# Padding the SBUF pools of a hybrid encoder block so that the tiles of its 128x512 matmuls start at multiples of 128 bytes

## The chip, the cores and the metric

The kernel runs on one core of one Trainium2 chip. The metric is the device time of that core in microseconds (us). The core's engines are TensorE (PE in the rows; its weight loads are listed as PEld), VectorE (DVE), ScalarE (ACT), GpSimd (POOL) and SyncE (SP, which here only issues transfers). Tiles live in SBUF, 128 partitions wide; a tile's address is the byte at which it starts in each partition, and that byte is what this change is about. Matmul results go to PSUM.

## What is computed

One layer of a streaming encoder over `x` of 2048 tokens and 1024 channels, all in float32 (cut):

```python
xn = rmsnorm(h, in_norm_g)
q, fz, v, gz, u = split(xn @ w_in)             # 2560 columns
o_hg = hgrn2_mix(q, fz, v, gz, lb, norm_g)     # gated linear recurrence, 4 heads, chunks of 64
o_s5 = s5_mix(u, ...)                          # 32 groups of a 64-state complex SSM, then a GLU of 512x512
h = h + concatenate([o_hg, o_s5]) @ w_out
hn = rmsnorm(h, ffn_norm_g)
hid = hn @ w_up                                # 1024 -> 2 * 2816
hid = conv_b + sum(shifted(hid, j) * conv_w[j] for j in range(3))
gate, val = split(hid)
h = h + (silu(gate) * val) @ w_down            # 2816 -> 1024
return rmsnorm(h, final_norm_g)
```

## The kernel before

**Matmuls.** Every large product is done in split precision: a float32 tile is written as a high part (`ACTIVATE`, line 121) and a low part (a subtraction, line 65), both of type `float32r`, and three matmuls replace one: high x high, high x low, low x high. Each of them is a 128x128 weight block against 512 moving columns. The program has 8,448 of these 128x512 matmuls. They are issued in one fixed order, and each loads its own weights:

```python
for kt in range(KT):                                         # project, lines 216 to 222
    a = wh[:, kt * P : (kt + 1) * P]                         # weights, high
    b = wl[:, kt * P : (kt + 1) * P]                         # weights, low
    xh, xl = xn[0][kt // 4][:, kt % 4], xn[1][kt // 4][:, kt % 4]
    PE.matmul(ps, a, xh, start=(kt == 0), stop=False)        # L220: weights, then moving tile
    PE.matmul(ps, a, xl, start=False, stop=False)            # L221
    PE.matmul(ps, b, xh, start=False, stop=(kt == KT - 1))   # L222
```

**Stages**, in order of time:

- *Projection and mixers* (0 to about 640 us). `project` (L220 to L222) makes 80 blocks of 24 matmuls: weights `wh`, `wl` of pool `wp`, moving tiles `xh`, `xl` of pool `xnp`. Between the blocks stand short float32 matmuls of the two mixers (L489, L574, L575, L637, L681, L700, L702 and others, up to 128 columns), with their DVE, ACT and POOL work and their transfers. The list `todo` ties each mixer step to a block ("slot").
- *GLU and output projection* (640 to 865 us). `glu_mm` (L886 to L888) has weights `wg` and moving tiles `g`, both in pool `wop`; `out_tile` (L963) has weights `ogp` and `zp` (pool `mx`) and moving tiles `wo` (pool `wop`), 16 tiles of 48 matmuls.
- *Up-projection with convolution* (about 870 to 1760 us). 44 units (2 token halves x 22 feature pairs) of seven Strassen-like products P1 to P7, 12 matmuls each, by `product` (L1162). The weights `uh`, `ul` (pool `fw`) are made while the unit before runs. The moving tiles are the token sums: P1 and P2 read `nh`, `nl` (pool `fa`), the other five read `tT1`, `tT2`, `tB22`, `tT3`, `tT4` (pool `fb`). In 40 units the order is P1, P5, P6, P2, P7, P3, P4, so that P5 (`tT1`) and P7 (`tT3`) stand right behind the two that read `nh`, `nl`.
- *Down-projection* (about 1770 to the end). 96 x 2 plain matmuls (`down`, L1466) and then 20 chunks of seven products of 24 matmuls (`one_product`, L1379): weights `gvh`, `gvl` (pool `fd`), moving tiles `dh`, `dl` (half of them in `fa`, half in `fd`). After each product DVE adds PSUM to the accumulator `accp` (line 62); behind that, in DVE's order, it makes the `gvl` and `dl` of the next chunk (line 65) from `graw`, which is loaded from `gv_d`.

**What sets addresses.** Tiles are taken from pools. A pool lies on the left (addresses rise) or, with `side="right"`, on the right, below the one opened before it. A tile takes its size, rounded up to 32 bytes, and there is no other rounding. So one odd-sized small tile shifts all that follows it in its pool, and the pools behind it. The right side starts at byte 229,344, which is 1,791 x 128 + 96: the four 4,096-byte buffers of `xp`, and what lies below them, start 96 bytes past a multiple of 128. The lines that matter:

```python
cp = ctx.enter_context(tc.tile_pool(name="cp", bufs=1))                       # 90
sm = ctx.enter_context(tc.tile_pool(name="sm", bufs=2))                       # 91
xp = ctx.enter_context(tc.tile_pool(name="xp", bufs=4, side="right"))         # 92
lbm = cs.tile([P, 4], F32, name="lbm")                                        # 303: 16 bytes, takes 32
sf = p3.enter_context(tc.tile_pool(name="sf", bufs=2))                        # 1272: small tiles, ahead of fd
```

## Time and profile before

| | us |
|---|---|
| three runs | 2249.85, 2245.22, 2246.74 (median 2246.74) |
| the profiled execution | 2248.36 |
| its span, first to last instruction | 2246.5 |
| PE busy in the span | 2163.2 (96%), 10,248 instructions |
| DVE busy | 1700.3 (76%) |
| ACT busy | 994.9 (44%) |
| POOL busy | 732.3 (33%) |
[...]

The span leaves 1.9 us of the profiled execution outside it. A PE that is busy 96% is not yet at its peak: the durations of matmuls overlap (a row gives about 0.39 us for a matmul whose successor starts after 0.23 us), so what a matmul costs is read from the distance between starts, or from a piece of the chain of waits, which counts no time twice.

### The profile page before, as it was taken

Reading aid. Unit: us, or ns where it says so; the run is one execution under the profiler, and the core shown is the slowest. Engines: PE = TensorE matmul, PEld = TensorE weight load, DVE = VectorE, ACT = ScalarE, POOL = GpSimd, SP = SyncE. Lnnn points to the kernel's source line nnn. Section 1 sums busy time; section 2 is a strip of 40 time slices with the busy share of each in tenths; the row PEclk is TensorE's granted clock in tenths of the full one; section 3 lists DMA queues with packets and bytes.
Section 4 is the critical chain, followed back from the end, with each engine's and each line's share of the span. In section 5 each row is a group of like instructions: output and inputs, shape, how many; then the busy total and the mean of one; then the engine's idle time right before and its main releaser. Section 6 shows DMA issues by size and latency. Waiting matters only on the chain.

```text
span 2246.5 us, 28693 instructions
## 1 busy us (share of the span) xinstructions
PE 2163.2 (96%) x10248; PEld 1745.3 (78%) x10248; DVE 1700.3 (76%) x2629; ACT 994.9 (44%) x1818; POOL 732.3 (33%) x666
## 2 busy tenths in 40 slices
PE   8999999999989998999999999999999889999996
PEld 6788887888878886888878877888888667777775
DVE  9998885666673336877778798777777788788888
ACT  5333462333363346655555564555555323232343
POOL 1111100000000001555455546565544245354433
PEclk9999999999999999999999999999999999999998
DMA  6566665354433357334324252222221622222223
GB/s 225 167 209 190 195 194 168 108 159 126 142 113 113 113 170 239 122 113 136 121 91 145 79 191 96 82 78 84 75 85 57 241 92 80 75 85 76 75 85 122
DMA packets 169519, 287.37 MB, mean 128 GB/s; under 512 B 46112, under 2 KB 85920, under 8 KB 169376
## 3 DMA queue, kind: packets, MB, share of 16 engines
q1 hardware_dynamic: 164624, 268.23, 37.0%
q0 software_dynamic: 4752, 17.30, 2.0%
q8 instruction: 81, 1.33, 0.2%
q14 instruction: 62, 0.51, 0.1%
HBM read 191.11 MB, written 94.37 MB: 127 GB/s over the span
## 4 chain that ended last, share of the span: by engine, by line
PE 70%; DVE 17%; DMA 5%; issue 4%; ACT 3%; SPq 1%; POOL 1%; DVEq 0%; POOLq 0%; ACTq 0%
PE ps_u L1162 18%; PE ps_v L1162 9%; PE ps_out L963 7%; PE ps_du L1379 5%; PE ps_w L1162 5%; PE ps_pj L220 5%; PE ps_pj L222 5%; PE ps_pj L221 5%; PE ps_dv L1379 3%; DVE accp L62 2%; DVE gvl L65 2%; DMA graw<-gv_d 2%; DVE dl L65 1%; PE ps_dn L1466 1%; DVE cv L74 1%
## 5 line engine op out<-in xcount | busy, mean ns | idle before, releaser
L220 PE MATMUL ps_pj<-xh,wh 128*128 128x512 f32 x640 | 261.9, 409 | 6.5 <-ACT xh L190 6.3
L222 PE MATMUL ps_pj<-xh,wl 128*128 128x512 f32 x640 | 255.1, 399 | 0.5 <-DMA wl<-ws_d 0.5
L221 PE MATMUL ps_pj<-xl,wh 128*128 128x512 f32 x640 | 255.5, 399 | 0.0
L74 DVE SCALAR_TENSOR_TENSOR cv<-cv,par 128x1024 f32<-128x1024 f32 x176 | 238.5, 1372 | 19.8 <-ACT cv L1174 17.8
L121 ACT ACTIVATE uh<-us 128x512 fp32r<-128x512 f32 x176 | 110.5, 629 | 183.2 <-PE ps_u L1162 87.8
L56 POOL TENSOR_TENSOR us<-uraw 128x512 f32<-128x512 f32 x86 | 122.1, 1420 | 186.7 <-DMA uraw<-in_wup_dram 170.0
L121 ACT ACTIVATE uh<-uraw 128x512 fp32r<-128x512 f32 x132 | 83.4, 632 | 159.7 <-PE ps_u L1162 84.4
L1379 PE MATMUL ps_du<-dh,gvh 128*128 128x512 f32 x320 | 131.6, 411 | 22.8 <-DVE accp L62 16.5
L65 DVE TENSOR_TENSOR ul<-us,uh 128x512 fp32r<-128x512 f32 x133 | 150.3, 1130 | 1.4 <-ACT uh L121 1.3
L220 PEld LDWEIGHTS ps_pj<-xh,wh 128*128 128x128 f32 x640 | 121.3, 189 | 37.2 <-ACT xh L190 6.3
L222 PEld LDWEIGHTS ps_pj<-xh,wl 128*128 128x128 f32 x640 | 121.1, 189 | 30.1 <-DMA wl<-ws_d 0.9
L221 PEld LDWEIGHTS ps_pj<-xl,wh 128*128 128x128 f32 x640 | 121.3, 190 | 26.9 <-DVE xl L74 0.9
L65 POOL TENSOR_TENSOR ul<-us,uh 128x512 fp32r<-128x512 f32 x43 | 72.8, 1692 | 174.4 <-ACT uh L121 174.4
L1379 PE MATMUL ps_du<-dl,gvh 128*128 128x512 f32 x320 | 127.9, 400 | 0.0
L1379 PE MATMUL ps_du<-dh,gvl 128*128 128x512 f32 x320 | 127.9, 400 | 0.0
L121 ACT ACTIVATE gvh<-gs 128x512 fp32r<-128x512 f32 x80 | 50.4, 630 | 161.6 <-POOL gs L56 77.0
L62 DVE TENSOR_TENSOR accp<-accp,ps_du 128x1024 f32<-128x1024 f32 (+1 forms) x84 | 97.7, 1163 | 28.0 <-PE ps_du L1379 27.7
L1174 ACT ACTIVATE cv<-cv,par 128x1024 f32<-128x1024 f32 x88 | 109.5, 1244 | 16.3 <-DVE cv L62 14.9
L56 POOL TENSOR_TENSOR gs<-graw 128x512 f32<-128x512 f32 x38 | 58.9, 1549 | 157.2 <-DMA graw<-gv_d 157.2
L963 PE MATMUL ps_out<-wo,ogp 128*128 128x512 f32 x384 | 100.2, 409 | 0.0
L1379 PEld LDWEIGHTS ps_du<-dh,gvh 128*128 128x128 f32 x320 | 61.5, 192 | 46.8 <-issue 23.1
L963 PE MATMUL ps_out<-wo,zp 128*128 128x512 f32 x384 | 92.7, 397 | 0.0
(431 smaller groups left out, 6024.8 us busy)
## 6 DMA issues: line engine op xcount, KB each, us to landing
uraw<-in_wup_dram SPq DMA_DIRECT2D x86, 512.0 KB
gv_d<-cv SPq DMA_DIRECT2D x43, 512.0 KB
graw<-gv_d SPq DMA_DIRECT2D x84, 256.0 KB
wraw<-in_win_dram SPq DMA_DIRECT2D x24, 512.0 KB
xt<-in_wdown_dram SPq DMA_DIRECT2D x44, 256.0 KB
ws_d<-wh POOLq DMA_DIRECT2D x16, 512.0 KB, 3.8
ws_d<-wl POOLq DMA_DIRECT2D x16, 512.0 KB, 5.7
wh<-ws_d SPq DMA_DIRECT2D x16, 512.0 KB
```

Source lines behind the costliest of these rows:

```text
L56: eng.tensor_tensor(o, a, b, op=op)
L62: eng.tensor_tensor(o, a, b, op=ALU.add)
L65: eng.tensor_tensor(o, a, b, op=ALU.subtract)
L74: eng.scalar_tensor_tensor(o, a, s, b, op0=op0, op1=op1)
L121: SC.activation(h, raw, AF.Copy)
L220: PE.matmul(ps, a, xh, start=(kt == 0), stop=False)
L221: PE.matmul(ps, a, xl, start=False, stop=False)
L222: PE.matmul(ps, b, xh, start=False, stop=(kt == KT - 1))
L963: PE.matmul(pss[nh], parts[lp][kt][:, tq], wo[rp][kt][:, nh * BLK : (nh + 1) * BLK], start=first, stop=last)
L1162: PE.matmul(ps, l, r[kt], start=(fresh and first), stop=end, skip_group_check=not fresh)
L1174: SC.activation(c, cin[:, 2 : HALF + 2], AF.Identity, scale=tap[2], bias=par[:, C_CB + cb : C_CB + cb + 1])
L1379: PE.matmul(ps[:, i], l[:, j, i * P : (i + 1) * P], r, start=(fresh and n == 0), stop=(n == 5), skip_group_check=not fresh)
```

## The change

Five small tiles that nobody reads or writes are allocated, one at each place where a pool would leave the multiples of 128. They are 96 bytes at the top of the right side, 64 in `sp`, 32 and 64 in `cs`, and 64 in `sf`. No other line changes.

```diff
+LINE, TOP = 128, 229344
+
+
 def _body(ctx, tc, A, out, dbg=None):
...
     sm = ctx.enter_context(tc.tile_pool(name="sm", bufs=2))
+    top = ctx.enter_context(tc.tile_pool(name="top", bufs=1, side="right"))
+    top.tile([P, (TOP - LINE * (TOP // LINE)) // 4], F32, name="pad")
     xp = ctx.enter_context(tc.tile_pool(name="xp", bufs=4, side="right"))
...
         sp = p1.enter_context(tc.tile_pool(name="sp", bufs=1, side="right"))
+        sp.tile([P, 16], F32, name="pad")
         hp = p1.enter_context(tc.tile_pool(name="hp", bufs=1, side="right"))
...
         lbn = cs.tile([P, 4], F32, name="lbn")
+        cs.tile([P, 8], F32, name="pad")
...
         r8 = cs.tile([P, PAIRS], F32, name="r8")
+        cs.tile([P, 16], F32, name="pad2")
         nci = cs.tile([P, PAIRS, 16], F32, name="nci")
...
         sf = p3.enter_context(tc.tile_pool(name="sf", bufs=2))
+        sf.tile([P, 16], F32, name="pad", bufs=1)
         fd = p3.enter_context(tc.tile_pool(name="fd", reuse_waits="tile", bufs=1))
```

No instruction moves: on each engine the built program has the same instructions in the same order with the same operands and shapes, and the same waits, but for one wait of POOL that is content with one ACT instruction fewer. Only addresses differ. The start of the 128x512 matmuls' operands, in bytes past a multiple of 128, as the two builds lay them out:

| line | matmuls | moving tile: before, after | weight block: before, after |
|---|---|---|---|
| L220, L221, L222 (projection) | 1,920 | 0, 0 | 32, 0 |
| L886 to L888 (GLU) | 192 | 0, 0 | 0, 0 |
| L963 (output projection) | 768 | 0, 0 | 96, 0 |
| L1162, P1 and P2 (`nh`, `nl`) | 1,056 | 96, 0 | 0, 0 |
| L1162, the other five products | 2,640 | 0, 0 | 0, 0 |
| L1379 (down-projection) | 1,680 | 64 or 96, 0 | 64, 0 |
| L1466 (plain down-projection) | 192 | 96, 0 | 64, 0 |

That L1162 has two rows is what makes it useful: 1,056 matmuls whose moving tile is off, and 2,640 with both operands on a multiple of 128, run in turn in the same stage. The short float32 matmuls of the mixers have operands at 32 or 96 before, and at 0 after in all but a few. The tiles of the convolution (`cv`, six buffers of 4,104 bytes) are not brought to multiples of 128, only shifted.

## Rows read from the trace of the kernel before

**Rows 1.** Windows, all engines: stretch, length, busy us (instructions) per engine, granted clock.

```profile
core 0: us, PE busy (x) PEld busy (x) DVE busy (x) ACT busy (x) POOL busy (x), PEclk, DMA share, GB/s
0.00:100.00 100.00, 86.28 (x396) 66.79 (x397) 90.41 (x332) 43.30 (x76) 13.77 (x49) 0.97 0.63 202
100.00:350.00 250.00, 248.27 (x1566) 204.15 (x1565) 221.98 (x565) 113.42 (x292) 26.64 (x71) 1.00 0.62 193
350.00:640.00 290.00, 286.46 (x1678) 236.04 (x1678) 185.09 (x430) 97.03 (x281) 3.65 (x17) 1.00 0.43 133
1360.00:1740.00 380.00, 379.15 (x1650) 309.54 (x1649) 284.32 (x257) 192.32 (x274) 206.48 (x156) 1.00 0.24 79
1820.00:2180.00 360.00, 345.97 (x1460) 275.07 (x1460) 300.09 (x321) 114.92 (x192) 157.16 (x102) 0.99 0.23 74
```

**Rows 2.** Waits of PE over the span: total us, times, longest.

```profile
PE ps_du L1379 <- DVE accp L62: 16.5, 18, 4.6
...
PE ps_u L1162 <- DVE cv L62: 5.4, 3, 3.7
...
PE ps_du L1379 <- DVE rs_t L59: 2.6, 1, 2.6
```

**Rows 3.** Chain of waits, 1400 to 1425 us: start, us, what.

```profile
1400.62 2.76 PE ps_u L1162 x12
1403.38 2.72 PE ps_v L1162 x12
1406.10 5.53 PE ps_u L1162 x24
...
1417.11 2.81 PE ps_w L1162 x12
```

**Rows 4.** Lines of PE, 700 to 760 us: xcount, busy us, mean ns.

```profile
L963 PE MATMUL ps_out<-wo,ogp 128*128 128x512 f32 x98 | 23.8, 396 | 0.0
...
L887 PE MATMUL ps_glu<-g,wg 128*128 128x512 f32 x22 | 8.6, 389 | 0.0
```

**Rows 5.** Chain of waits, 640 to 830 us.

```profile
703.96 22.49 PE ps_out L963 x96
```

**Rows 6.** Timeline of PE, 560 to 567 us: start, us, instruction.

```profile
563.52 0.39 PE L221 MATMUL ps_pj<-xl,wh 128*128 128x512 f32 x1
...
566.78 0.40 PE L220 MATMUL ps_pj<-xh,wh 128*128 128x512 f32 x1
```

**Rows 7.** Timeline of PE behind a short wait, 1341.9 to 1345.3 us.

```profile
1342.31 0.50 PE L1162 MATMUL ps_u<-tT3h,uh 128*128 128x512 f32 x1
1342.65 0.40 PE L1162 MATMUL ps_u<-tT3l,uh 128*128 128x512 f32 x1
...
1345.21 0.40 PE L1162 MATMUL ps_u<-nh,uh 128*128 128x512 f32 x1
```

**Rows 8.** Windows of L221 alone: stretch, length, busy us (instructions) of PE, PEld.

```profile
100.00:350.00 250.00, 95.58 (x241) 45.18 (x240) 1.00 0.62 193
350.00:640.00 290.00, 117.10 (x296) 55.71 (x296) 1.00 0.43 133
```

**Rows 9.** Chain of waits, 1896 to 1926 us.

```profile
1898.38 5.55 PE ps_du L1379 x24
```

**Rows 10.** Chain of waits, 2082 to 2104 us.

```profile
2082.22 3.34 DMA graw<-gv_d
...
2088.03 1.23 DVE gvl L65
...
2094.57 3.00 PE ps_du L1379 x12
```

**Rows 11.** Chain of waits, 2170 to 2181 us.

```profile
2176.22 4.56 PE ps_du L1379 x12
```

**Rows 12.** Lines of ACT, 900 to 2180 us: xcount, busy us, mean ns.

```profile
L121 ACT ACTIVATE uh<-us 128x512 fp32r<-128x512 f32 x169 | 106.1, 629 | 179.7 <-PE ps_u L1162 87.8 <-PE ps_w L1162 68.1 <-PE ps_v L1162 23.6
...
L121 ACT ACTIVATE gvh<-gs 128x512 fp32r<-128x512 f32 x75 | 47.3, 631 | 156.1 <-POOL gs L56 73.0 <-PE ps_du L1379 35.1 <-DVE gs L56 22.8
```

## The prediction

> **What bounds the kernel now.** I read the windows first. PE is busy 248.27 of 250 us in the second part of the projection stage, 286.46 of 290 in its third and 379.15 of 380 in the up-projection; DVE, the next engine, is busy 89%, 64% and 75% there [rows 1]. Then the list of PE's waits: in a span of 2246.5 us the longest entry is 16.5 us, for DVE's accumulation in the down-projection, and the up-projection's largest is 5.4 us [rows 2]. So over most of the time the end is set by how fast PE starts one matmul after the other. A change of addresses moves no instruction; what it can change is the distance between two starts.

> That distance is in the chain of waits, where a piece with a count holds so many matmuls back to back. In the up-projection the trace compares addresses by itself, since P1 and P2 read `nh`, `nl` (96 bytes past a multiple of 128) and the rest read tiles that lie on one. The 12 matmuls of P2 (`ps_w`) take 2.81 us, 234.2 ns each. The 12 of P3 (`tB22`, the `ps_v` piece) take 2.72 us, 226.7 ns each. P7, right behind P2, reads `tT3`, which lies on a multiple of 128, and takes 2.76 us, 230.0 ns each (the first `ps_u` piece) [rows 3]. I read the last as an after-effect: starts that fell out of step take most of a product to fall back in. Of 24 matmuls in one piece (P4, then P1 of the next unit) 5.53 us are 12 x 226.7 + 12 x 234.2 [rows 3], so the two prices add up.

> Weights count too. In the output projection and GLU all moving tiles are on multiples of 128, and weights are on one for L887 but 96 past one for L963: mean durations 389 and 396 ns [rows 4], and 96 matmuls of L963 take 22.49 us, 234.3 ns each [rows 5]. Projection, weights 32 past: 14 distances from 563.52 to 566.78 us, 232.9 ns each [rows 6]. Down-projection, both operands off: 24 in 5.55 us, 231.2 ns [rows 9]. Every group with an operand off costs 231 to 234 ns, the groups with none 226.7. I take 226.7 ns as the price after.

> **The change part by part.** It adds no work, so the sum is one of gains, matmuls x (price now - 226.7 ns), cut where PE does not set the pace.

> *Up-projection.* P1 and P2: 2 x 12 x 44 = 1,056 matmuls x 7.5 ns = 7.9 us. P5 and P7 lose their after-effect: 12 x (230.0 - 226.7) = 40 ns, in some 82 products, 3.3 us. PE sets the pace here (379.15 of 380 us, [rows 1]). A unit gets shorter by 2 x 90 + 2 x 40 = 0.26 us of 19.3, 1.3%, and DVE at 75% covers that. I take 11.0 of 11.2, for the few products at the start that wait.

> *Output projection.* 768 matmuls x (234.3 - 226.7) = 5.8 us. The last quarter is woven with transposes and waits for transfers; I count 592 matmuls in full (4.5 us) and 0.3 for the rest: 4.8.

> *Projection.* Each block of 24 follows short float32 matmuls. Behind a break the next starts are slow even with both operands on multiples of 128: the first distance is 0.34 us, and from 1342.65 to 1345.21 us follow 11 of 232.7 ns [rows 7]. So only the later 12 of 24 gain, 12 x 6.2 = 74 ns a block. From 350 us on, 296 / 8 = 37 blocks [rows 8]: 2.7 us, kept, with DVE at 64%. From 100 to 350 us, 241 / 8 = 30 blocks, 2.2 us; DVE is 89% busy, so I keep 1.4. Before 100 us PE is busy 86 and DVE 90 [rows 1], and PE follows loads and splits: 0. Together 4.1.

> *Down-projection.* Of a chunk's 84 matmuls some 22 stand behind one of two breaks; 62 x (231.2 - 226.7) = 0.28 us, times 20 = 5.5 us. Here another loop is close. `graw` is loaded (3.34 us) after DVE has released its buffer, then POOL, ACT and DVE work on it, and PE waits for the accumulation queued behind that in DVE's order [rows 10]. Where a chunk has this stall, a faster PE only waits longer, and there are 18 such waits over the 20 chunks [rows 2]. I keep a little under half, 0.45 x 5.5 = 2.4, for the chunks between two stalls in which DVE has caught up. The 192 plain matmuls: 192 x 4.5 = 0.9, kept.

> *Short float32 matmuls.* 632 starts of 128 columns with operands off. If the price goes with columns, 7.5 / 4 = 1.9 ns each, 1.2 us; if it is per start, 4.7; if nothing, 0. I take 0.8, near the first, since part lies under DVE.

> *Other engines.* ACT's split takes 629 ns for tiles on a multiple of 128 (`uh`) and 631 for tiles 64 past one (`gvh`) [rows 12]: no price there, so I cost ACT, DVE and POOL at 0. I have no row that sets a load's address against its duration. The 3.34 us of `graw` [rows 10] bound it: a tenth more or less in some 15 loads on the chain is 5 us either way. I take 0, as the loads' bytes stay the same.

> **The sum:** 11.0 + 4.8 + 4.1 + 2.4 + 0.9 + 0.8 = 24.0 us. The profiled execution takes 2248.36 us, with a span of 2246.5; the forecast of its like is 2224.4, and since the median of the runs lies 1.6 us below it, 2222.7 for the median, a gain of 1.1%. Ends of the unknown costs: with everything kept and no after-effect left anywhere (11.2 + 5.8 + 1,920 x 6.2 ns + 1,680 x 4.5 ns + 0.9 + 4.7) the gain is 42 us, 2205. With the up-projection at 9, the output projection at 4.3, 1 from the projection and nothing else it is 14.3, 2232.4; the loads' 5 us may shift either end.

> **A rule against the change.** [...]

> **The rivals.**

> *The distances come from something else than the start byte* (which other tiles or engines are at work in P1 and P2, or the stretch of SBUF). Then nothing changes: 2246.7. For it: the price after is read from tiles that differ in more than their residue. Against: weights alone off (L963) and moving tiles alone off (P1, P2) show the same 234 ns in two stages, and L887 runs between L963's tiles in the same 60 us. I give it 8%, with the rule above in it, which would give the same.

> *DVE takes over.* In the projection up to 350 us and in the chunks, DVE is at 89% and 83% [rows 1]. If it absorbs all that PE gains there, and a fifth of the up-projection's gain, in units where a wait on `cv` [rows 2] becomes the later one: 24.0 - 1.4 - 2.4 - 2.2 - 0.8 = 17.2, and with the output projection at 4.3 and the plain matmuls at 0 it is 15.8: 2231. 17%.

> *More is kept.* If blocks behind a break fall into step at once when their own tiles are in order, the projection gives 67 x 24 x 6.2 ns = 10.0 instead of 4.1, and the chunks 0.7 of 84 x 4.5 ns x 20 = 5.3 instead of 2.4: 24.0 + 5.9 + 2.9 = 32.8, 2214. 14%.

> *Slower: the clock.* [...] 4%.

> **How the numbers follow.** My forecast, 2222.7, with its own range of 2217 to 2229, gets 57%; nothing changes 8%, DVE takes over 17%, more is kept 14%, slower 4%. The range that should hold the time 8 times in 10 takes in both neighbours: 2210 to 2236. About 0.2% (4.5 us) is what a measurement of this kernel tells from no change. Faster by more than that: 57 + 17 + 14 = 88%; within it: 8%; slower: 4%.

> **What would show it.** In the chain after, pieces of 12 in the up-projection should all read 2.72 us, `ps_w` too, and 96 of L963 about 21.8. In the projection blocks the later distances should be 227 ns and the first ten still 233. PE's waits for `accp` should grow by 2 to 4 us in total. PEclk and the durations of ACT and DVE should stay. The prediction is wrong in its mechanism if `ps_w` stays at 2.81, wrong in its cover if `ps_w` falls and the up-projection's units keep 19.3 us, and wrong in its size if the projection's 80 blocks gain over their whole length.

## The result and the profile after: half of the forecast

The changed kernel takes 2237.86 us (median of five runs, 2234.42 to 2239.54). The kernel before, now with five runs, takes 2249.79 us (2245.22 to 2251.27). The ratio is 0.995, with a 95% interval of 0.9935 to 0.9966. It is faster by 11.9 us, half of the 24 that were forecast, and 2237.86 lies outside the range that ended at 2236. The forecast stood on a median of three runs, 2246.74; with five it is 3 us higher, so the gain says more about the miss than the time does. The two profiled executions have spans of 2246.5 and 2237.4 us: 9.1 us, which the rest of this text follows by stage.

Where both operands of a matmul kind stand at the same place, the step of the prediction is there. The chain of waits of the changed kernel in the up-projection (start, us, what) answers to [rows 3]; `ps_w`, 2.81 us before, and P7 behind it, 2.76, now read as all others do:

```profile
1392.20 2.72 PE ps_w L1171 x12
1394.92 2.72 PE ps_u L1171 x12
1397.64 2.72 PE ps_v L1171 x12
1400.37 5.44 PE ps_u L1171 x24
```

So does the output projection, in the same view; before, 96 of these took 22.49 us [rows 5]:

```profile
700.73 21.76 PE ps_out L972 x96
```

The projection and the down-projection did not follow. For the projection, the timeline of PE (start, us, instruction) shows the same 14 distances as [rows 6]: 3.25 us, 232 ns each, where the kernel before had 233.

```profile
561.55 0.39 PE L228 MATMUL ps_pj<-xl,wh 128*128 128x512 f32 x1
...
564.80 0.39 PE L227 MATMUL ps_pj<-xh,wh 128*128 128x512 f32 x1
```

In the down-projection the chain has 24 matmuls in 5.53 us, against 5.55 [rows 9]. These are two products: one has 12 matmuls there, not 24, which makes 84 in a chunk.

```profile
1887.31 5.53 PE ps_du L1389 x24
```

The windows of the changed kernel (columns as in [rows 1]) give the stages. PE is as close to its limit as before, and the granted clock (0.987 of full speed over the span before, 0.986 after) and the shares of DVE and ACT have hardly moved, so the place to look is the distance between starts and what PE waits for:

```profile
100.00:350.00 250.00, 247.49 (x1567) 204.20 (x1566) 221.59 (x564) 112.92 (x292) 26.49 (x70) 1.00 0.60 193
350.00:640.00 290.00, 284.79 (x1673) 235.83 (x1671) 186.48 (x430) 97.08 (x281) 5.29 (x17) 1.00 0.42 132
1360.00:1740.00 380.00, 379.00 (x1673) 313.48 (x1672) 290.69 (x261) 196.02 (x280) 220.00 (x154) 1.00 0.25 83
1820.00:2180.00 360.00, 350.78 (x1484) 278.58 (x1482) 301.50 (x322) 119.57 (x200) 154.04 (x98) 0.99 0.23 78
```

Since the two programs issue the same 10,248 PE instructions in the same order, the gain can be followed from one to the next: the start of PE instruction number n before, less its start after, is the lead at that place. Its growth by stage, in us:

| stage (times of the kernel before) | forecast | in the traces |
|---|---|---|
| to the first L963 (645) | 4.1 + 0.8 | 2.1 |
| output projection (645 to 845) | 4.8 | 4.5 |
| turn to the up-projection (845 to 870) | 0 | 0.9 |
| up-projection, first half, units 0 to 21 (870 to 1326) | 5.5 | -2.5 |
| up-projection, second half, units 22 to 42 (1326 to 1737) | 5.5 | 5.3 |
| unit 43 and plain down-projection (1737 to 1811) | 0.9 | 1.6 |
| down-projection, chunks (1811 to the end) | 2.4 | -2.8 |
| sum | 24.0 | 9.1 |

The first row is the least certain: two other programs with the same addresses up to there led by 2.7 us (e4 below) and by 0.4 (e9). Three places are to be explained: the projection, the first half of the up-projection, and the chunks.

### The profile page after: what moved, and what is told of

The parts are those of the page before. It is cut to its first block, busy times and chain, and to the rows that moved or that the text cites. A ratio compares the mean times of both kernels' runs of the same rounds, so it can differ in the third digit from the quotient of the medians.

```text
span 2237.4 us, 28693 instructions
## 1 busy us (share of the span) xinstructions
PE 2147.7 (96%) x10248; PEld 1744.9 (78%) x10248; DVE 1702.5 (76%) x2629; ACT 995.3 (44%) x1818; POOL 756.7 (34%) x666
## 4 chain that ended last, share of the span: by engine, by line
PE 68%; DVE 17%; DMA 5%; issue 4%; ACT 4%; SPq 1%; POOL 1%; DVEq 0%; POOLq 0%; ACTq 0%
PE ps_u L1171 18%; PE ps_v L1171 9%; PE ps_out L972 6%; PE ps_du L1389 5%; PE ps_pj L227 5%; PE ps_pj L229 5%; PE ps_pj L228 5%; PE ps_w L1171 5%; PE ps_dv L1389 3%; DVE accp L66 2%; DMA graw<-gv_d 2%; DVE gvl L69 2%; PE ps_dn L1476 2%; DVE cv L78 1%; DVE dl L69 1%
## 5 line engine op out<-in xcount | busy, mean ns | idle before, releaser
L227 PE MATMUL ps_pj<-xh,wh 128*128 128x512 f32 x640 | 260.9, 408 | 6.5 <-ACT xh L197 6.2
L78 DVE SCALAR_TENSOR_TENSOR cv<-cv,par 128x1024 f32<-128x1024 f32 x176 | 247.7, 1424 | 24.0 <-ACT cv L1183 22.4
L229 PE MATMUL ps_pj<-xh,wl 128*128 128x512 f32 x640 | 254.2, 397 | 0.0
L60 POOL TENSOR_TENSOR us<-uraw 128x512 f32<-128x512 f32 x86 | 128.0, 1489 | 188.3 <-DMA uraw<-in_wup_dram 143.2
L1389 PE MATMUL ps_du<-dh,gvh 128*128 128x512 f32 x320 | 130.6, 408 | 24.2 <-DVE accp L66 16.7
L69 DVE TENSOR_TENSOR ul<-us,uh 128x512 fp32r<-128x512 f32 x133 | 150.4, 1131 | 1.4 <-ACT uh L127 1.3
L227 PEld LDWEIGHTS ps_pj<-xh,wh 128*128 128x128 f32 x640 | 121.3, 190 | 36.4 <-ACT xh L197 6.3
L229 PEld LDWEIGHTS ps_pj<-xh,wl 128*128 128x128 f32 x640 | 121.1, 189 | 28.4 <-issue 0.7
L1389 PE MATMUL ps_du<-dh,gvl 128*128 128x512 f32 x320 | 128.8, 403 | 0.0
L1389 PE MATMUL ps_du<-dl,gvh 128*128 128x512 f32 x320 | 128.5, 402 | 0.0
L69 POOL TENSOR_TENSOR ul<-us,uh 128x512 fp32r<-128x512 f32 x43 | 73.2, 1703 | 154.2 <-ACT uh L127 137.8
L1389 PEld LDWEIGHTS ps_du<-dh,gvh 128*128 128x128 f32 x320 | 61.5, 192 | 48.7 <-issue 24.0
```

Source lines behind the costliest of these rows:

```text
L60: eng.tensor_tensor(o, a, b, op=op)
L69: eng.tensor_tensor(o, a, b, op=ALU.subtract)
L78: eng.scalar_tensor_tensor(o, a, s, b, op0=op0, op1=op1)
L1389: PE.matmul(ps[:, i], l[:, j, i * P : (i + 1) * P], r, start=(fresh and n == 0), stop=(n == 5), skip_group_check=not fresh)
```

## The experiments

Distances are means over all neighbouring 128x512 matmuls of a line whose starts lie less than 245 ns apart, so that waits and the stretches at the lower clock (granted 0.50, starts 427 ns apart) are left out.

**What about an address sets the distance?** Three theories. A: only the difference of the two operands' addresses counts, modulo 256 bytes; it must be zero. B: a multiple of 128 is enough, and projection and down-projection are held up by something else. C: each operand's own remainder counts. They can be told apart because the changed kernel's operands, taken modulo 512, still differ: moving tile and weights both stand at 384 in the up-projection and the output projection, but at 384 and 256 in the projection, and at 256 or 384 against 256 in the down-projection.

*First run (e1_equal): two of the five pads grow by 128 bytes*, so that every operand stands at 384 of 512.

```diff
-        cs.tile([P, 16], F32, name="pad2")
+        cs.tile([P, 48], F32, name="pad2")
...
-        sf.tile([P, 16], F32, name="pad", bufs=1)
+        sf.tile([P, 48], F32, name="pad", bufs=1)
```

> The changed kernel with 128 bytes more ahead of the pool wp and ahead of the pool fd, so that in every 128x512 matmul the moving tile and the weight block start at the same remainder of 512 (384 in all). Theory A (what counts is that the two operands start at equal remainders, not that each lies on a multiple of 128): the matmuls of the projection (L227 to L229) fall from 232.5 ns apart to 226.7 after the first ten of each block of 24, those of the down-projection (L1389) from 231.8 to about 227.5 on average; the projection gains 2 to 4 us, the down-projection 1 to 3 more, and the time is 2231 to 2235 us. Rival B (a multiple of 128 is enough, and something else holds the projection and the down-projection at 232): both stay at 232, time as the changed kernel, 2238.

Measured: 2228.29 us (2226.90 to 2230.14), ratio 0.9902 (0.9888 to 0.9915) against a kernel before of 2250.36. The projection falls to 227.8 to 228.5 ns, the down-projection to 227.1, the plain one to 226.9. The chain of this kernel in the down-projection, and its timeline over the 14 distances shown above, where the first eight take 231 ns each and the last six 226.7:

```profile
1882.98 5.44 PE ps_du L1389 x24
```

```profile
558.98 0.39 PE L228 MATMUL ps_pj<-xl,wh 128*128 128x512 f32 x1
...
560.83 0.39 PE L227 MATMUL ps_pj<-xh,wh 128*128 128x512 f32 x1
...
562.19 0.39 PE L227 MATMUL ps_pj<-xh,wh 128*128 128x512 f32 x1
```

So 128 bytes between the operands cost some 10 us (2237.86 - 2228.29 = 9.6). B falls.

*Second run (e2_equal_odd): the same, and everything shifted by 32 bytes*, so that all operands stand at 416 of 512 and none lies on a multiple of 64 or 128.

```diff
-    top.tile([P, (TOP - LINE * (TOP // LINE)) // 4], F32, name="pad")
+    top.tile([P, 16], F32, name="pad")
...
+    cp.tile([P, 8], F32, name="pad")
```

> The kernel of the run before, with every tile of SBUF moved up by 32 bytes, so that no operand of a 128x512 matmul lies on a multiple of 128 or 64 any more, but all still at one remainder of 512 (416). Theory A (equal remainders): every group at 226.7 ns as in the run before, time the same within 3 us. Rival C (what counts is the remainder of each operand by itself, be it 0 of 128 or 128 of 256): all groups at 231 to 235 ns, so the up-projection alone is 3,696 x 7 ns = 26 us slower than in the run before, time above 2255 us.

Measured: 2228.54 us (2227.19 to 2229.61), ratio 0.9902 (0.9889 to 0.9916). All lines are within 0.4 ns of the first run. In its chain of waits:

```profile
750.87 21.76 PE ps_out L973 x96
```

C falls, and with it the change's own reason: multiples of 128 have no part in it.

*Third run (e3_offsets): the first run, with the token sums 256 bytes and the down-projection's weights 64 bytes away from their partners.*

```diff
+        fb.tile([P, 64], F32, name="pad")
...
+        fd.tile([P, 16], F32, name="pad")
```

> The kernel with equal remainders, with 256 bytes put ahead of the five token sums of the up-projection and 64 ahead of the weight tiles of the down-projection: P5, P6, P7, P3 and P4 now have moving tile and weight block 256 bytes apart (of 512), P1 and P2 stay equal; in L1391 they are 64 apart. Theory A with a period of 256: the five products stay at 226.7 ns. Theory A with a period of 512: they go to 231 to 235 ns, and so do most of P1 and P2's neighbours. In the down-projection 64 apart should give 231 to 234 under theory A, and 226.7 under a rule that asks only for multiples of 64. Rival B: nothing differs between the stages and the changed kernel.

Measured: one run, 2234.76 us. 256 bytes cost nothing (226.7 to 227.3 ns in the five products that read the token sums, 226.8 to 227.3 in the changed kernel), 64 bytes cost 6 ns (233.3 in the down-projection). The chain of this kernel, a `ps_u` piece of the up-projection whose first half reads token sums, and a piece of the down-projection:

```profile
1395.84 5.44 PE ps_u L1171 x24
...
1882.57 5.60 PE ps_du L1391 x24
```

That leaves A, with a period of 256 bytes among the distances tried. All of them together:

| operands apart, modulo 256 | where | ns from start to start |
|---|---|---|
| 0 | up-projection and output projection after; the same and the down-projection in e1 and e2 | 226.8 to 227.2 |
| 0, with breaks between blocks | projection of e1 to e3 | 227.7 to 228.5 |
| 256, hence 0 | token sums of e3 | 226.7 to 227.3 |
| 32 | projection before (weights ahead); plain down-projection before (moving tile ahead) | 233.2; 233.3 |
| 64 | down-projection of e3 | 233.3 |
| 96 | output projection before (weights ahead); P1 and P2 before (moving tile ahead) | 234.2; 234.3 to 234.6 |
| 128 | projection after | 232.4 to 232.6 |

One observation has to be fitted in. In the chunks of the changed kernel half of the matmuls (852 of 1,680) have equal remainders, and yet the distance behind them is 232.5 ns, against 231.2 behind the others, which are 128 apart. (The kernel before has the same weave, with 32 in place of 128: 231.3 and 231.5.) Most of them stand in groups of three between groups of three, and falling into step takes longer than that. Where 12 to 18 follow each other (nine stretches, one of them with starts 427 ns apart), the last distances do come to 226 or 227 in the changed kernel too. This is such a stretch of 15, in the timeline of PE: ten distances of 231 ns, then four of 227.

```profile
1906.13 0.39 PE L1389 MATMUL ps_dv<-dh,gvh 128*128 128x512 f32 x1
...
1908.44 0.39 PE L1389 MATMUL ps_du<-dl,gvh 128*128 128x512 f32 x1
...
1909.35 0.39 PE L1389 MATMUL ps_du<-dh,gvl 128*128 128x512 f32 x1
```

*Fourth run (e5_right_only): the changed kernel with three of its five pads taken out again.*

```diff
-        cs.tile([P, 8], F32, name="pad")
...
-        cs.tile([P, 16], F32, name="pad2")
...
-        sf.tile([P, 16], F32, name="pad", bufs=1)
```

> The changed kernel without three of its five pads (the two ahead of the projection's weights and the one ahead of the down-projection's tiles); the two on the right side stay. Projection: moving tiles at 384, weights at 160 bytes past a multiple of 512 again, as in the kernel before; down-projection: weights at 192, moving tiles at 192 or 384. Theory A (only the two operands' equal remainder of 256 counts): these three pads brought nothing, because they left 128 bytes between the operands; 2238 to 2240 us, the projection at 233.2 ns a start, the down-projection at 231.5 to 232, up-projection and output projection still 226.9. The prediction's step (a multiple of 128 is what counts): 4.1 + 2.4 + 0.9 + 0.8 = 8.2 us are lost, 2246 us.

Measured: 2238.71 us (2235.69 to 2241.29), ratio 0.9952 (0.9936 to 0.9968). That can't be told from the changed kernel's 0.995: the three pads were worth nothing measurable, where the prediction had 8.2 us for them. The projection is back at 233.1 to 233.3 ns, the chunks are at 231.7 (231.8 with the pads).

**Where did the gain of the first half go?** The lengths of the units of the up-projection, from the start of a unit's first matmul to the next one's, show it. The columns of the last four kernels are used further below.

| unit | before | after | before, held | after, held | e1 | e1, held |
|---|---|---|---|---|---|---|
| 5, 9, 13, 17 to 20 (each) | 19.31 | 19.04 | 19.31 | 19.04 | 19.04 | 19.04 |
| 2 | 19.31 | 19.04 | 19.56 | 19.33 | 19.04 | 19.33 |
| 6, 10, 14 | 19.31 each | 19.04 each | 20.03, 19.88, 19.88 | 19.04 each | 19.04 each | 19.04 each |
| 3 | 21.09 | 21.16 | 21.82 | 21.74 | 20.86 | 21.79 |
| 4 | 20.41 | 20.68 | 19.33 | 19.22 | 20.49 | 19.26 |
| 7 | 21.09 | 20.91 | 21.62 | 21.53 | 20.86 | 21.56 |
| 8 | 20.44 | 20.82 | 19.81 | 19.40 | 20.84 | 19.59 |
| 11 | 21.29 | 21.17 | 21.71 | 21.28 | 21.18 | 21.39 |
| 12 | 21.26 | 23.01 | 19.33 | 19.34 | 23.32 | 19.41 |
| 15 | 21.06 | 21.17 | 21.66 | 21.46 | 20.86 | 21.41 |
| 16 | 19.33 | 19.62 | 19.33 | 19.43 | 19.62 | 19.62 |
| sum, 2 to 16 | 301.1 | 301.8 | 301.9 | 297.0 | 301.3 | 297.6 |
| 0 and 1 together | 54.0 | 55.6 | 54.0 | 55.8 | 55.4 | 55.1 |
| 21 | 23.26 | 24.61 | 24.15 | 24.01 | 24.61 | 24.59 |

The plain units lose 0.27 us, where 0.26 was forecast. Four units grew by 0.3 to 1.75 us instead, 4, 8, 12 and 16, each behind a unit in which tokens of the second half are transposed. There PE's second product over `ps_u`, P6, waits until ACT has copied out the first. The list of PE's waits from 955 to 1220 us, before and after (us in all, times, longest):

```profile
PE ps_u L1162 <- ACT cv L1186: 3.3, 3, 1.7
```

```profile
PE ps_u L1171 <- ACT cv L1195: 5.1, 4, 2.0
```

What stands ahead of that copy is in the chain of waits around unit 12. Before:

```profile
1121.03 3.85 DMA xt<-h_d
...
1125.52 0.80 ACT xt L986 x2
1126.32 1.13 ACT cv L1174
...
1131.57 0.59 ACT cv L1186
1132.16 0.04 issue
1132.20 3.02 PE ps_u L1162 x12
```

And after:

```profile
1114.98 4.22 DMA xt<-h_d
...
1119.23 0.51 ACT xt L995
1119.74 1.13 ACT cv L1183
...
1124.99 0.59 ACT cv L1195
1125.58 0.04 issue
1125.62 4.63 PE ps_u L1171 x12
```

Read it from the top. In both kernels ACT ran seven of the eight scalings of the next rows (`xt`, L995 after, L986 before) ahead of the convolution and of the copy of `ps_u`, and it stood idle for the transfer of these rows, 2.8 us before and 2.9 after. The transfer in turn came behind DVE's work on the row buffers (the last step on `xt` ends at 1116.97 us before and 1110.28 after) and behind SP, which issued eight of them, at most 0.61 us each. From the start of unit 11 to the start of that copy it is 28.05 us before (1103.5 to 1131.57) and 28.16 after (1096.8 to 1124.99). PE got through its part earlier and waited longer, 2.04 us before and 2.41 after from the last start ahead of the wait to the first one behind it (the list above counts the idle time alone). And behind the longer wait the product itself took 4.63 us instead of 3.02. The windows of these 4 us (the granted clock is the number behind POOL) show why, after and then before: 0.59 against 1.00. From 1127 to 1130 us it was 0.50.

```profile
1126.00:1130.00 4.00, 4.00 (x12) 3.17 (x11) 3.90 (x3) 0.71 (x3) 2.50 (x3) 0.59 0.01 2
```

```profile
1132.20:1136.20 4.00, 4.00 (x17) 3.30 (x18) 3.90 (x3) 2.07 (x4) 3.35 (x4) 1.00 0.01 2
```

Two limits of this reading. The fall of the clock in unit 12 is not steady: in e4 starts are 427 ns apart there too, and in e1 the unit takes 23.32 us, but in e2, whose operands are at one remainder here as well, a wait of 2.65 us at the same place was followed by a product of 3.01 us (below), as short as the 3.02 us before at a clock of 1.00, and unit 12 took 21.59 us. And unit 16 is another case. The rows come in four groups, loaded in units 0, 3, 7 and 11, so no scaling stands ahead of its copy; in the chain there ACT waits 1.9 us for DVE's convolution.

```profile
1121.41 3.01 PE ps_u L1172 x12
```

*Fifth run (e4_scale_late): the changed kernel, the scaling written two steps later in the code.*

```diff
                     dma(xt[:, i], h_d[t * P : (t + 1) * P, :].rearrange("p (k q c) -> p k q c", k=2, q=4)[:, :, q])
-                    SC.activation(xt[:, i], xt[:, i], AF.Copy, scale=rst[:, t : t + 1])
                 x.append(xt)
 
         def turned(j):
             b.append(halves(x_tile()))
+            for i in range(4):
+                t = 8 * hf + 4 * j + i
+                SC.activation(x[j][:, i], x[j][:, i], AF.Copy, scale=rst[:, t : t + 1])
```

> The changed kernel, with one edit in the up-projection's woven units: the eight ACT scalings of the rows loaded from h_d stand no longer right behind the loads (where ACT, in order, waits for the transfer, and PE waits for ACT to empty PSUM), but at the head of the transposes, most of a unit later. Theory D (these waits took the up-projection's gain in the first token half: 1.71, 1.85, 2.41 and 0.68 us ahead of P6 in four units, and 1.6 us of half clock behind the third): they vanish or fall under 0.5 us each, the first half gets 4 to 7 us shorter, time 2231 to 2235 us. Rival E (the units wait for the loads wherever the scaling stands, since the transposes need them): the waits move to the transposes, time 2236 to 2240.

Measured: 2236.00 us (2233.19 to 2238.39), ratio 0.9935 (0.9921 to 0.9949), an interval that overlaps the changed kernel's. The waits stayed, 5.4 us in the same stretch. A miss, but of the edit: in the built program, whose order a scheduler sets, the scaling stands at nearly the same place as before, in the unit of the transposes before it. The theory was not put to the test.

*Sixth to eighth run: a dependence that holds the scaling back.* DVE makes a copy of the eight scaling factors at the end of units 1, 5, 9 and 13, from a tile of that unit times zero, and the scaling reads that copy. Then it can't run before, and by that time the rows should have arrived: in the changed kernel those of unit 11 landed at 1119.2 us, and unit 13 ended at 1160.0. The same edit goes into the kernel before (e8_before_hold), the changed one (e9_after_hold) and the first run's (e10_equal_hold):

```diff
+            late[q] = fb.tile([P, 8], F32, tag=f"late{q}", name="late")
+            stt(late[q], W3["cv"][:, BLK + 2 : BLK + 10], 0.0, rst[:, 8:16], ALU.mult, ALU.add)
...
-                    SC.activation(xt[:, i], xt[:, i], AF.Copy, scale=rst[:, t : t + 1])
+                    SC.activation(xt[:, i], xt[:, i], AF.Copy, scale=late[q][:, 4 * j + i : 4 * j + i + 1] if hf else rst[:, t : t + 1])
...
+                elif hf == 0 and f % 4 == 1 and f < 18:
+                    weave = {"P4": [lambda q=f // 4: later(q)]}
```

> The kernel before, with one thing added: ACT's scaling of the second half's rows reads its factors from a copy that DVE makes at the end of units 1, 5, 9 and 13 of the up-projection, so that it can't stand in ACT's queue one unit earlier, ahead of the PSUM copies of units 4, 8, 12 and 16, while the rows are still on their way. Theory F (these four units are set by the chain of loads through ACT's queue, not by PE): units 4, 8, 12 and 16 fall from 20.41, 20.44, 21.26 and 19.33 us to 19.31 each, 4.2 us in all: 2246 beside a kernel before at 2250. Theory G (DVE's sums and splits set them, ACT is only the last to be seen): the four units stay within 0.3 us, and so does the time within 2 us.

> The same addition to the changed kernel. Theory F: units 4, 8, 12 and 16 fall from 20.68, 20.82, 23.01 and 19.62 us to 19.04 each, 8.0 us in all: 2230. Against the kernel before with the same addition that is a gain of 16, where the change alone gained 12: the 4 us that the first half of the up-projection swallowed come out. Theory G: units unchanged, 2238.

> The kernel with all operands at one remainder (384 of 512), with the same addition. Theory A and F together: 2228.3 less 20.49 + 20.84 + 23.32 + 19.62 - 4 x 19.04 = 8.1 us gives 2220, since what the two do lies in different stretches. If F falls: 2228.

Measured, against a kernel before of 2249.6 us:

| kernel | us | ratio (95%) |
|---|---|---|
| before, held | 2248.56 (2244.87 to 2254.26) | 0.9993 (0.9982 to 1.0005) |
| after, held | 2234.96 (2233.41 to 2238.76) | 0.9936 (0.992 to 0.9951) |
| e1, held | 2223.14 (2222.16 to 2224.44) | 0.9882 (0.9864 to 0.9901) |

The long waits are gone. What the list of PE's waits has left from 955 to 1220 us, in the kernel before and in the changed one, both held:

```profile
PE ps_x L994 <- ACT xt L996: 1.2, 3, 0.4
PE ps_u L1163 <- ACT cv L1188: 1.1, 4, 0.4
```

```profile
PE ps_x L1003 <- ACT xt L1005: 1.0, 3, 0.5
```

And in the chain around unit 12 of the changed kernel, held, PE stands behind PE alone:

```profile
1121.54 2.72 PE ps_v L1172 x12
1124.26 0.01 issue
1124.27 3.01 PE ps_u L1172 x12
1127.28 2.72 PE ps_w L1172 x12
```

The table of units is a two by two. Without the hold, the change brings units 2 to 16 nothing, 301.1 to 301.8 us (300.0 to 302.0 in the changed kernel and e1 to e5); with it, they get shorter, 301.9 to 297.0 (297.6 in e10). That is 4.9 us where 15 x 0.27 = 4.05 were to be had; 1.9 of it are units 6, 10 and 14, where the hold costs the kernel before something. Taking the scaling out of the way is worth 4.9 us to the changed kernel and nothing to the kernel before, so ACT's queue took the gain of these units. The forecast of the whole was still missed: 8.0 us were expected of the hold in the changed kernel, and units 4, 8, 12 and 16 did give 6.7 of them (84.13 to 77.39), but units 2, 3, 7, 11 and 15 got 1.9 us longer. Unit 2 is one of those in which the scaling is now done; in the other four PE's transposes (`ps_x`) wait for ACT's copy of them. In the kernel before this went further, 4.4 us, with units 6, 10 and 14 among them, where the scaling is done too, against 3.6 gained; the hold is worth nothing there. Why those three lose only in that kernel was not traced.

By the spans, the change is worth 9.1 us without the hold and 12.6 with it (2246.5 to 2233.9); the intervals of the two ratios overlap, so it is the units that show this, not the medians. Both edits together with the equal remainders make the fastest kernel, 2223.14 us, 1.2% below the kernel before; the hold's share of it is 5 us by the medians, of 8 expected. The intervals of the two ratios overlap here too; the units 2 to 16 give 3.7 of it (301.3 to 297.6).

Units 0, 1 and 21 are not explained by this. Units 0 and 1 together got 1.5 us longer in this pair of profiles, but in the other kernels with the changed up-projection they take anything from 54.0 (e2) to 56.5 us (e5). Unit 21 got 1.35 us longer; it takes 24.6 us in all the changed kernels but e9, where it is 24.0, and the hold alone lengthens it from 23.3 to 24.2 in the kernel before. PE waits there for DVE: for its splits of the token sums (L65 before, L69 after) in unit 0, 4.6 us before and 4.4 after, and for its `cv` in unit 21, 3.7 us before and 4.1 after in the list of waits. So DVE seems to set the pace; nothing was run to show it.

**And the chunks?** In the down-projection the lead is about 12 us, with swings of 1 us from 1838 us on, until the last chunk, where 2.6 us are lost at one place. The chain of waits there, before and after:

```profile
2209.97 1.14 DVE accp L62
2211.25 4.41 PE ps_du L1379 x18
```

```profile
2198.42 1.14 DVE accp L66
2199.70 6.97 PE ps_du L1389 x18
```

Both products start behind a wait for DVE's accumulation, from start to start 1.85 us before and 4.29 after; the earlier wait of the same chunk is about 4 us in both (3.98 and 4.03). Before, the clock fell behind the earlier one, while PE had time in hand; after, it fell behind the later one, where PE is last. The granted clock of the two products, after and then before:

```profile
2200.00:2205.00 5.00, 5.00 (x13) 3.83 (x13) 1.89 (x3) 2.19 (x4) 0.00 (x0) 0.50 0.38 151
```

```profile
2211.30:2215.30 4.00, 4.00 (x18) 3.25 (x19) 3.13 (x4) 2.20 (x4) 0.00 (x0) 1.00 0.54 214
```

And of the products behind the earlier wait, after and then before:

```profile
2190.00:2194.00 4.00, 3.97 (x17) 3.30 (x18) 3.93 (x6) 3.08 (x4) 1.84 (x1) 1.00 0.26 105
```

```profile
2201.60:2205.60 4.00, 4.00 (x10) 3.13 (x11) 3.93 (x6) 2.71 (x3) 1.89 (x1) 0.50 0.28 112
```

In e1 the two waits are 4.09 and then 1.53 us, the 12 matmuls behind the later one take 3.00 us, and its last chunk loses nothing. What decides which of the two waits the fall follows was not tested.

## Why the prediction was half right, step by step

- *226.7 ns is the price with both operands in order; the change reaches it in every group.* Right where it was read from, the up-projection and the output projection (226.9 ns in both). Wrong in the projection and the down-projection, and this is the step that failed first. The prediction compared groups "with an operand off" and groups "with none", and every group with none was also one whose two operands had equal remainders. Remainders modulo 128 could not show the difference; modulo 512 they do, and the table of operands could have been drawn up that way beforehand. By it the projection goes from 32 bytes apart to 128, and half of the chunks' matmuls, read as "both operands off", were never apart. After the change a start costs 232.5 ns in the projection and 231.8 in the chunks. With equal remainders throughout the two stages do gain: the lead at 645 us is 4.6 to 7.1 in e1, e2, e3 and e10 (forecast 4.1 + 0.8), and the chunks get 4.1 to 5.6 us shorter in e1, e2 and e10 (forecast 2.4).
- *The after-effect.* Right: P5 and P7 now take 2.72 us. Also right that the first starts behind a break stay slow: in the projection of e1 the second to tenth distance of a block average 232 falling to 228 ns, and the later ones 226.8 to 227.6.
- *"A unit gets shorter by 0.26 us of 19.3, and DVE at 75% covers that."* The size was right in the second half and in the plain units of the first (0.27). The cover was not, and this is the second step that failed: a mean share of busy time said nothing of ACT, whose queue held PE behind a transfer in units 4, 8 and 12, nor of the waits for DVE at the start and the turn. "I take 11.0 of 11.2" came to 2.8.
- *The rival that DVE takes over* had the right shape, a wait that swallows a part of the up-projection's gain, but named DVE alone where units 2 to 16, which lost 4.8 us against the forecast, lost it to ACT's queue, and gave a fifth of the gain where three quarters went.
- *Output projection:* 4.8 forecast, 4.5 found. *Plain matmuls:* 0.9 forecast from prices that were not theirs (233.3 ns before, 232.3 after, which is 0.2 us); of the 1.6 us found there 0.2 are unit 43's, and the rest lies at the start of the plain matmuls, where PE has waits (2.8 and 2.5 us, the same in both kernels) and the lower clock in both (0.51 from 1765 to 1770 us before, 0.68 from 1755 to 1760 after). *Short float32 matmuls:* 0.8 forecast; no run sets them apart from the rest of the projection.
- *Chunks:* the mechanism named, a faster PE only waits longer, was not put to the test by the change, since PE got no faster (231.8 ns, 231.4 before); the waits for `accp` stayed, 16.7 us against 16.5 [rows 2], and the loss is the clock's. Where PE did get faster there, the forecast growth of 2 to 4 us did not come: the waits are 13.6 us in e1, 15.1 in e2 and 14.8 in e10 (they scatter: 14.2 in e5, where PE was as slow as before). The chunks kept 4.1 to 5.6 us there, so 0.45 of 5.5 was too small a share. The two lines are the changed kernel's and e1's. The slower rival did not come. Before, a product behind a wait lost 1.8 us at the lower clock: 4.56 us [rows 11] against 12 x 0.231 = 2.77, at 0.50 from 2177 to 2179 us. In the changed kernel's profile such a loss came anew once in unit 12 (4.63 us against 3.02) and once where it cost more than before, in the last chunk (6.97 against 4.41).

```profile
PE ps_du L1389 <- DVE accp L66: 16.7, 17, 3.9
```

```profile
PE ps_du L1389 <- DVE accp L66: 13.6, 13, 3.2
```

- *The rival that the start byte doesn't matter:* it does matter, and differences of 32, 64, 96 and 128 bytes cost 6 to 8 ns a start (232.4 to 234.6 against 226.7). The rule that is in its 8% is shown by no run.
- *The loads and the other engines at 0:* ACT's split of `us` takes 629 ns before and after. DVE's step of the convolution (`cv`, whose tiles only shifted) has a mean of 1,372 ns before and 1,424 after, but a median of 1,280 and 1,284; the tail grows in the held kernel before as well (mean 1,404), so it is not shown to be the addresses. A price of the loads' addresses was not looked for.

## To carry to other kernels

Look at the two operands of a matmul together: pads that put the moving tile and the weights at the same remainder of 256 bytes are worth some 3% of a 512-column float32r matmul here (226.7 to 227.3 ns a start against 232.4 to 234.6), and the three pads that brought operands to multiples of 128 but left them 128 bytes apart were worth nothing measurable (2237.86 us with them, 2238.71 without). Before a small gain per loop round is multiplied by the number of rounds, list the rounds by length: those that were longer than the plain ones were set by something else here, and in unit 12 the gain turned into a longer wait (2.04 to 2.41 us) with a slower product behind it (3.02 to 4.63 us). To move a step in a program whose order is set by a scheduler, give it a dependence, since its place in the code may not count.
